# mLSTM stage: both parts of u are loaded from DRAM, where the pooling stage stores them, and the gates' bias is an eighth part of the gates' sum

## The chip, the cores and the metric

One core of a Trainium2 chip runs the program in one launch; times are device microseconds (us) of that core. TensorE (PE) multiplies, VectorE (DVE), ScalarE (ACT) and GpSimd (POOL) work on elements, and SyncE (SP) issues most of the DMA transfers. SBUF is the memory on the chip from which the engines read, PSUM the one into which PE writes.

## What is computed

A decoder layer over 4096 positions of width 1024. One normalised input u feeds two branches, a pooling mixer and an mLSTM with four heads; their outputs are joined, projected and added to x, and a last norm follows.

```python
def rmsnorm(x, w):
    y = x * lax.rsqrt(jnp.mean(x * x, axis=-1, keepdims=True) + EPS)
    return y * w

u = rmsnorm(x, norm_w)
proj = u @ w_in                      # 1024 x 5120: pool_x, pool_z, m_x, m_z, m_o
y_pool = pool_mixer(pool_x, pool_w, pool_scale) * silu(pool_z)
# mLSTM branch
xc = silu(causal_conv(m_x, conv_w, conv_b))
q, k, v = headwise(xc, w_q), headwise(xc, w_k), headwise(m_x, w_v)
gates = concatenate([q, k, v], -1) @ w_if + b_if     # 4 input and 4 forget gates
h = mlstm_chunkwise(q, k, v, i_pre, f_pre)           # chunks of 128, state C, n, m carried
y_mlstm = (head_norm(sigmoid(m_o) * h) * mh_norm_w + m_skip * xc) * silu(m_z)
out = rmsnorm(x + concatenate([y_pool, y_mlstm], -1) @ w_out, final_norm_w)
```

## The kernel before, in words

Products are taken in three matmuls each. A float32 operand is split into a high part, rounded to fp32r, and a low part, what is left (`split`, L104 casts on ACT and L105 subtracts, on DVE where no other engine is named), and `mm3` (L111 to L113) adds high by high, high by low and low by high.

The work has three parts in time.

*The pooling stage* goes through 8 blocks of 512 positions. For each block `norm_u` loads x transposed (x_t, L404), sums squares, has PE spread the norm (L419, L436) and stores the normalised x as float32 into the DRAM tensors us_d (L444), by quarters that later passes read. `make_u` splits it into the tiles u, eight pairs of a high and a low part, from a pool of 19 buffers. Eight steps j per block multiply u by two sets of weights (L111 to L113, `acc<-u,w`); the product is pooled, gated and stored to yp_d (L568). SP issues all these loads and stores in the order of its queue, and an issue waits there for the data it stores.

*The mLSTM stage* begins with its projection weights, eight pairs of loads of 256 KB with their splits (`ws`, L605), and with small products of the block-diagonal maps. Then `project(b)` computes m_x for sub-blocks of 256 positions, 16 of them. It loads the normalised x from us_d (L739, four loads of 256 KB) into tiles xu, casts the high part on ACT (L741) and subtracts on POOL (L742), in place. The pool xu has 12 tiles, of which one sub-block takes 8. The convolution and SiLU (`tail`, L678, L700 to L704) follow, and xc is stored to xc_d (L704).

`front` prepares a chunk of 128 positions: three products for v and its share of the gates (L779), each emptied by a split into va (L104, L105) and a reduction into `part` (L782); two maps for q and k (L789, copied by L791); two of scores (L800, emptied by L803 and L805); two transposes (L811). All of these take their PSUM from one ring of four buffers named `map`, in the order in which they are written. The gates g are the sum of the seven shares in `part` (L815) plus the bias `bif` (L816); ACT turns them into ef (L818 to L820), DVE into lf (L822), and PE transposes lf and g (L825, L826). `back` does the heads: it splits scaled rows into ws (L893 on ACT, L894 on DVE), multiplies by va and by the split state cs (L907, L911), stores h (L925 on ACT into ht, of which there is one buffer; L928) and updates the state c (L936, added by L937; its split on ACT and POOL is L665 and L666).

A string ORDER for even and one for odd chunks gives the order in which steps of `front`, `back`, `project` and `tail` are written. The framework's scheduler then orders the instructions of each engine by its own estimates, so a change of one instruction can move others. Two chunks, with one sub-block of `project`, make a period.

*The passes* after that form the output gate, the SiLU gate and the output projection (L1100 and later); the change leaves their code alone.

Of the kernel before, what the change touches and what calls it, by code (L numbers as in the profile page):

```python
# [8 lines left out]
F32 = mybir.dt.float32  # L9
F32R = mybir.dt.float32r  # L10
BF16 = mybir.dt.bfloat16
AF = mybir.ActivationFunctionType
ALU = mybir.AluOpType
# [4 lines left out]
P = 128  # L18
D = 1024
NJ = D // P  # L20

T = 512
# [5 lines left out]
TB = 256  # L28
# [12 lines left out]
A_OF = ("a11", "s2", "a12", "s3", "s1", "a22", "s4", "a21")  # L41
# [13 lines left out]
def tile_hybrid(  # L55
# [16 lines left out]
    nc = tc.nc  # L72
    S = x.shape[0]
    NB = S // T
# [5 lines left out]
    dram = ctx.enter_context(tc.tile_pool(name="dram", bufs=1, space=DRAM))  # L80
# [14 lines left out]
    us_d = [dram.tile([NP + 1, P, 4, T], F32, name=f"us_d{r}") for r in range(NR)]  # L95
    yp_d = [dram.tile([NP + 1, P, 4, T], F32, name=f"yp_d{r}") for r in range(NR)]
    ym_d = [dram.tile([NP, P, 4, T], F32, name=f"ym_d{r}") for r in range(NR)]
    xc_d = [dram.tile([NJ, P, T], F32, name=f"xc_d{b}") for b in range(NB)]
    h_d = [dram.tile([NCH, P, D], F32, name=f"h_d{b}") for b in range(NB)]

# [275 lines left out]
    def proj_t(ps, wpair, u):  # L376
        mm3(ps, [(kcol(wpair, k), u[k]) for k in range(NJ)])


    with tc.tile_pool(name="a_st", bufs=4) as stp, \  # L380
# [66 lines left out]
        def make_u(xs):  # L447
            u = []
            for k in range(NJ):
                hi = up.tile([P, T], F32R, name="u")  # L450
                lo = up.tile([P, T], F32R, name="u")
                split(xs[k // 2][:, k % 2], hi, lo)
                u.append((hi, lo))
            return u
# [70 lines left out]
        u = make_u(xs)  # L525
        job = None
        jobs = []
        for b in range(NB):
            if b % 2:
                jobs += [(us_d[b // 2], k) for k in (0, 2)]  # L530
            elif b:
                jobs += [(yp_d[b // 2 - 1], k) for k in (0, 2)]
            if b + 1 == NB:
                jobs += [(p_out1, k) for k in (0, 2)]
            for j in range(NJ):
                g = j // 2
                win = WINDOWS[g]
                ps = accp.tile([P, T], F32, name="acc")
                o = (j % 2) * P
                mm3(ps, [(tuple(t[:, k * 256 + o:k * 256 + o + P] for t in wz[g]), u[k]) for k in range(NJ)])  # L540
                z = wk.tile([P, HALO + T], F32, name="z")
                nc.scalar.copy(out=z[:, HALO:], in_=ps)
                nc.gpsimd.tensor_copy(out=z[:, 0:HALO], in_=halo[:, j, :])
                nc.gpsimd.tensor_copy(out=halo[:, j, :], in_=z[:, T:])
                pz = accp.tile([P, T], F32, name="acc")
                proj_t(pz, wg[j], u)
                sg = wk.tile([P, T], F32, name="sg")
                last_silu = nc.scalar.activation(out=sg, in_=pz, func=AF.Silu)

                cur, lo_c, step = z, 0, 1  # L550
                while step < win:
                    nxt = one.tile([P, HALO + T], F32, name=f"sum{(step.bit_length()) % 2}")
                    a = lo_c + step
                    nc.vector.tensor_tensor(out=nxt[:, a:], in0=cur[:, a:], in1=cur[:, a - step:HALO + T - step],
                                            op=ALU.add)
                    cur, lo_c, step = nxt, a, step * 2
                dlt = cur[:, HALO:]
                if b == 0:
                    n = win - 1
                    fix = wk.tile([P, HALO], F32, name="fix")  # L560
                    nc.vector.tensor_tensor(out=fix[:, :n], in0=cur[:, HALO:HALO + n], in1=inv0[:, :n], op=ALU.mult)
                nc.vector.scalar_tensor_tensor(out=dlt, in0=cur[:, HALO:], scalar=1.0 / win, in1=z[:, HALO:],
                                               op0=ALU.mult, op1=ALU.subtract)
                if b == 0:
                    nc.vector.tensor_tensor(out=dlt[:, :n], in0=fix[:, :n], in1=z[:, HALO:HALO + n], op=ALU.subtract)
                nc.vector.tensor_tensor(out=sg, in0=dlt, in1=sg, op=ALU.mult)
                quarter = A_OF.index(f"a{b % 2 + 1}{j // 4 + 1}")
                nc.sync.dma_start(out=yp_d[b // 2][quarter][:, j % 4, :], in_=sg)  # L568
                if b == 0 and j % 2 == 0 and g + 1 < H:
                    load_group(g + 1)  # L570
                if j == 0 and b + 1 < NB:
                    norm = norm_u(b + 1)
                if jobs and j in JOBS_AT[b + 1 == NB]:
                    dst, k = jobs.pop(0)
                    job = right_sums(dst, k) if dst is p_out1 else sums(dst, k)
                    next(job)
                elif job:
                    job = next(job, None)
                if j in NORM_AT[b > 0] and b + 1 < NB:
                    xs = next(norm)  # L580
            if b + 1 < NB:
                u = make_u(xs)
# [3 lines left out]
    with tc.tile_pool(name="b_mx", bufs=NJ) as mxp, \  # L586
# [7 lines left out]
        def x_tile(dt=F32):  # L594
            return xu.tile([P, T], dt, name="xu")

        def ws_tile():
            return wsp.tile([P, T], F32, name="ws")

        wm = [[w1p.tile([P, 4, T], F32R, name="w1") for _ in range(2)] for _ in range(4)]  # L600
        for i in range(4):
            for k in range(4):
                raw = ws_tile()
# [25 lines left out]
                                pattern=[[1, P]], channel_multiplier=-1)  # L629
        bif = one.tile([P, 8], F32, name="bif")  # L630
        nc.sync.dma_start(out=bif, in_=b_if.partition_broadcast(P))


        bvg = one.tile([P, NJ, GW], F32, name="bvg")
# [96 lines left out]
        def project(b):  # L731

            u = []
            for k in range(0, NJ, 2):
                lo = x_tile(F32R).rearrange("p (k l) -> p k l", k=2)
                raw = lo.bitcast(F32)
                l0 = b % 2 * TB
                quarter = A_OF.index(f"a{b // 2 % 2 + 1}{k // 4 + 1}")
                nc.sync.dma_start(out=raw, in_=us_d[b // 4][quarter][:, k % 4:k % 4 + 2, l0:l0 + TB])  # L739
                hi = x_tile(F32R).rearrange("p (k l) -> p k l", k=2)  # L740
                nc.scalar.copy(out=hi, in_=raw)  # L741
                nc.gpsimd.tensor_tensor(out=lo, in0=raw, in1=hi.bitcast(F32), op=ALU.subtract)  # L742
                u += [(hi[:, i], lo[:, i]) for i in range(2)]
            yield
            mx, xc = [], []
            for j in range(0, NJ, 2):
                ps = (accp if b or j % 4 else mmp).tile([P, 2, TB], F32, name="acc" if b or j % 4 else "mm")
                for i in range(2):
                    for part in range(2):
                        proj_part(ps[:, i], j + i, u, part)  # L750
                        if (i, part) != (1, 1):
                            yield
                m = mxp.tile([P, 2, 3 + TB], F32, name="mx", bufs=5)
                nc.gpsimd.tensor_copy(out=m[:, :, 0:3], in_=mhal[:, j:j + 2, :])
                nc.scalar.copy(out=m[:, :, 3:], in_=ps)
                nc.gpsimd.tensor_copy(out=mhal[:, j:j + 2, :], in_=m[:, :, TB:])
                a = mxp.tile([P, 2, TB], F32, name="xc", bufs=6)
                for t in range(2):
                    jj = j + t
                    nc.scalar.activation(out=a[:, t], in_=ps[:, t], func=AF.Identity,  # L760
                                         scale=conv_w[:, jj * 4 + 3:jj * 4 + 4], bias=conv_b[:, jj:jj + 1])
                tails.append(tail(b, j, m, a))
                mx += [m[:, i] for i in range(2)]
                xc += [a[:, i] for i in range(2)]
                if j + 2 < NJ:
                    yield
            return mx, xc

        def front(n, c, mx, xc):
            l0 = c * P  # L770
# [1 line left out]
            for t, one_ in zip(va, (1.0, 0.0)):  # L772
                nc.gpsimd.memset(t.bitcast(F32)[:, :, P:], one_)
            xs = st() if n + 1 < NB * NCH else None
            part = wk.tile([P, 8, 7], F32, name="part")
            for w, (j0, nj) in enumerate(((0, 3), (3, 3), (6, 2))):
                ps = mapp.tile([P, 3, GW], F32, name="map")
                for i in range(nj):
# [16 lines left out]
            for q in range(2):  # L795
                ps = mapp.tile([P, 2, GW], F32, name="map")
                for hh in range(2):
                    for t in range(2):
                        j = 4 * q + 2 * hh + t
# [4 lines left out]
                                        in1=causal.unsqueeze(1).broadcast_to([P, 2, P]), op=ALU.mult)  # L804
# [8 lines left out]
                yield  # L813
            g = wk.tile([P, 8], F32, name="g")
            nc.vector.tensor_reduce(out=g, in_=part, axis=AX.X, op=ALU.add)  # L815
            nc.vector.tensor_tensor(out=g, in0=g, in1=bif, op=ALU.add)  # L816
            ef = wk.tile([P, H], F32, name="ef")
            nc.scalar.activation(out=ef, in_=g[:, H:], func=AF.Abs)  # L818
            nc.scalar.activation(out=ef, in_=ef, func=AF.Exp, scale=-1.0)
# [55 lines left out]
            for h in range(H if n else 0):  # L875
                q = wk.tile([P, 2, 2, P], F32R, name="qi", bufs=4)
                raw = wk.tile([P, 2, P], F32, name="qr", bufs=4)
                nc.vector.tensor_tensor(out=raw, in0=qg[:, 2 * h:2 * h + 2, 0:P],
                                        in1=inter[:, h:h + 1, :].broadcast_to([P, 2, P]), op=ALU.mult)
# [426 lines left out]
```

## Time and profile before

| what | value |
|---|---|
| median of 3 runs | 3108.35 us (3103.76 to 3109.62) |
| profiled execution, its own time | 3106.23 us |
| its span | 3104.5 us |
| PE busy, mean granted clock | 2903.6 us (94%), 0.972 |
| DVE, ACT, POOL busy | 2116.8, 1352.9, 883.5 us |
| DMA | 531.59 MB, mean 171 GB/s |
| pooling stage | 0 to about 751 us |
| start of the mLSTM stage | about 751 to 815 us |
| mLSTM stage, steady part and end | about 815 to 1720 us |
| passes | to the end |

A row of waits reads: engine and line that waited, the engine and line that released it, then the total, the number and the longest wait in us. A row of the timeline is a start in us, a duration, the engine, the line and the tiles, and in brackets the idle time ahead of it. Rows of windows give the busy time of PE, of its weight loads, of DVE, ACT and POOL, then the granted clock, the DMA engines' share and GB/s.

### The profile page before, as it was taken

How to read it: one execution, taken by the hardware profiler on the slowest of the kernel's cores; microseconds unless marked ns; L12 is line 12 of the kernel's file. 1: busy time of each engine (PE TensorE's matmuls, PEld its weight loads, DVE VectorE, ACT ScalarE, POOL GpSimd, SP SyncE). 2: the span in 40 equal slices, each digit the busy share in tenths (PEclk: the TensorE clock that was granted, in tenths of full speed). 3: DMA queues.
4: the chain of work that ended last, by engine and by line, in shares of the span. 5: the costliest groups of instructions: out<-in, count | busy, mean ns of one | idle time of the engine just before them, and what ended most of it. 6: DMA issues, size and time to landing. Idle time of an engine off the chain costs nothing. (4 is left out here: it accounts for less than half of the span.)

```text
span 3104.5 us, 45002 instructions
## 1 busy us (share of the span) xinstructions
PE 2903.6 (94%) x15912; PEld 2520.3 (81%) x15912; DVE 2116.8 (68%) x4172; ACT 1352.9 (44%) x2658; POOL 883.5 (28%) x924
## 2 busy tenths in 40 slices
PE   7999999998899999999998898998999999989998
PEld 6888888887889989989997676886777778867887
DVE  6555555554688888888889644567667766676666
ACT  4222122221676676767767311245556633343332
POOL 1122333333244454444443231002011133220000
PEclk9999999998999999999999999999999999999999
DMA  6344455546221121111212788676677888886664
GB/s 214 113 158 157 160 186 187 186 149 199 82 67 50 49 69 49 61 57 48 66 59 92 250 281 288 218 256 218 228 238 247 268 270 279 277 285 207 202 210 169
DMA packets 258002, 531.59 MB, mean 171 GB/s; under 512 B 28528, under 2 KB 72048, under 8 KB 257776
## 3 DMA queue, kind: packets, MB, share of 16 engines
q1 hardware_dynamic: 225952, 412.84, 38.4%
q10 hardware_dynamic: 31824, 115.88, 12.2%
q8 instruction: 125, 2.05, 0.3%
q14 instruction: 101, 0.83, 0.1%
HBM read 331.49 MB, written 197.13 MB: 170 GB/s over the span
## 5 line engine op out<-in xcount | busy, mean ns | idle before, releaser
L111 PE MATMUL ps<-w,sr 128*128 128x512 f32 x1320 | 523.5, 397 | 27.0 <-ACT sr L104 18.5
L113 PE MATMUL ps<-w,sr 128*128 128x512 f32 x1320 | 520.4, 395 | 18.5 <-DVE sr L105 18.5
L112 PE MATMUL ps<-w,sr 128*128 128x512 f32 x1320 | 521.1, 395 | 0.0
L105 DVE TENSOR_TENSOR sr<-sr 128x1024 fp32r<-128x1024 f32 x221 | 284.9, 1292 | 302.2 <-ACT sr L104 301.5
L104 ACT CAST sr<-sr 128x1024 fp32r<-128x1024 f32 x221 | 231.2, 1047 | 535.0 <-PE ps L112 255.3
L111 PE MATMUL acc<-u,w 128*128 128x512 f32 x1024 | 399.3, 390 | 1.6 <-ACT u L104 1.6
L112 PE MATMUL acc<-u,w 128*128 128x512 f32 x1024 | 399.3, 390 | 0.0
L113 PE MATMUL acc<-u,w 128*128 128x512 f32 x1024 | 399.2, 390 | 0.0
L111 PEld LDWEIGHTS ps<-w,sr 128*128 128x128 f32 x1320 | 252.3, 191 | 82.2 <-ACT sr L104 22.3
L113 PEld LDWEIGHTS ps<-w,sr 128*128 128x128 f32 x1320 | 251.3, 190 | 74.5 <-DVE sr L105 22.2
L111 PE MATMUL acc<-xu,w 128*128 128x256 f32 x992 | 296.4, 299 | 0.0
L112 PEld LDWEIGHTS ps<-w,sr 128*128 128x128 f32 x1320 | 251.7, 191 | 52.4 <-issue 0.5
L113 PE MATMUL acc<-xu,w 128*128 128x256 f32 x992 | 283.3, 286 | 0.0
L112 PE MATMUL acc<-xu,w 128*128 128x256 f32 x992 | 283.3, 286 | 0.0
L666 POOL TENSOR_TENSOR cs<-c,cs 128x516 fp32r<-128x516 f32 x124 | 179.8, 1450 | 240.0 <-ACT cs L665 214.4
L678 DVE SCALAR_TENSOR_TENSOR xc<-mx,col,xc 128x256 f32<-128x256 f32 x384 | 226.2, 642 | 15.2 <-ACT xc L760 11.5
L111 PEld LDWEIGHTS acc<-u,w 128*128 128x128 f32 x1024 | 192.3, 188 | 42.3 <-ACT u L104 2.4
L113 PEld LDWEIGHTS acc<-u,w 128*128 128x128 f32 x1024 | 192.4, 188 | 40.1
L112 PEld LDWEIGHTS acc<-u,w 128*128 128x128 f32 x1024 | 192.4, 188 | 40.0
L111 PEld LDWEIGHTS acc<-xu,w 128*128 128x128 f32 x992 | 192.7, 194 | 1.2
L112 PEld LDWEIGHTS acc<-xu,w 128*128 128x128 f32 x992 | 192.8, 194 | 0.0
L113 PEld LDWEIGHTS acc<-xu,w 128*128 128x128 f32 x992 | 192.2, 194 | 0.1
(230 smaller groups left out, 5927.9 us busy)
## 6 DMA issues: line engine op xcount, KB each, us to landing
sr<-us_d ACTq DMA_DIRECT2D x112, 512.0 KB, 5.1
us_d<-st SPq DMA_DIRECT2D x64, 512.0 KB, 2.7
sr<-ym_d ACTq DMA_DIRECT2D x56, 512.0 KB, 4.3
sr<-yp_d ACTq DMA_DIRECT2D x53, 512.0 KB, 5.6
st<-in_x_t_dram SPq DMA_DIRECT2D x32, 512.0 KB, 6.0
yp_d<-sg SPq DMA_DIRECT2D x64, 256.0 KB, 2.9
st<-us_d SPq DMA_DIRECT2D x32, 512.0 KB, 5.9
xu<-us_d SPq DMA_DIRECT2D x64, 256.0 KB, 3.6
```

The costliest lines, as they stand in the source:

```text
L104: nc.scalar.copy(out=hi, in_=raw)
L105: (eng or nc.vector).tensor_tensor(out=lo, in0=raw, in1=hi.bitcast(F32), op=ALU.subtract)
L111: nc.tensor.matmul(ps, lhsT=a[0], rhs=b[0], start=start and k == 0, stop=False, skip_group_check=skip)
L112: nc.tensor.matmul(ps, lhsT=a[0], rhs=b[1], start=False, stop=False, skip_group_check=skip)
L113: nc.tensor.matmul(ps, lhsT=a[1], rhs=b[0], start=False, stop=stop and k == n - 1, skip_group_check=skip)
L666: nc.gpsimd.tensor_tensor(out=t[:, 1], in0=cst[h], in1=t[:, 0].bitcast(F32), op=ALU.subtract)
L678: nc.vector.scalar_tensor_tensor(out=a[:, t], in0=m[:, t, i:i + TB], scalar=conv_w[:, jj * 4 + i:jj * 4 + i + 1], in1=a[:, t], op0=ALU.mul ...
```

## The change

The pooling stage stores both parts of u to new DRAM tensors ub_d, one pair of stores for each j, behind the store of yp_d: 128 stores of 256 KB. `project` loads both parts from there, eight loads of 256 KB per sub-block in place of four; the cast L741 and the subtraction L742 are gone. `part` becomes two tiles that stay, used by even and odd chunks, with an eighth column that holds the bias, written once; the addition L816 is gone and L815 sums eight shares. us_d is still stored, since passes read it.

```diff
--- before.py
+++ after.py
@@ -95,6 +95,8 @@
     us_d = [dram.tile([NP + 1, P, 4, T], F32, name=f"us_d{r}") for r in range(NR)]
     yp_d = [dram.tile([NP + 1, P, 4, T], F32, name=f"yp_d{r}") for r in range(NR)]
     ym_d = [dram.tile([NP, P, 4, T], F32, name=f"ym_d{r}") for r in range(NR)]
+
+    ub_d = [dram.tile([2, P, NJ, T], F32, name=f"ub_d{b}") for b in range(NB)]
     xc_d = [dram.tile([NJ, P, T], F32, name=f"xc_d{b}") for b in range(NB)]
     h_d = [dram.tile([NCH, P, D], F32, name=f"h_d{b}") for b in range(NB)]
 
@@ -566,6 +568,8 @@
                 nc.vector.tensor_tensor(out=sg, in0=dlt, in1=sg, op=ALU.mult)
                 quarter = A_OF.index(f"a{b % 2 + 1}{j // 4 + 1}")
                 nc.sync.dma_start(out=yp_d[b // 2][quarter][:, j % 4, :], in_=sg)
+                for i in range(2):
+                    nc.sync.dma_start(out=ub_d[b][i][:, j, :], in_=u[j][i].bitcast(F32))
                 if b == 0 and j % 2 == 0 and g + 1 < H:
                     load_group(g + 1)
                 if j == 0 and b + 1 < NB:
@@ -629,6 +633,10 @@
                                 pattern=[[1, P]], channel_multiplier=-1)
         bif = one.tile([P, 8], F32, name="bif")
         nc.sync.dma_start(out=bif, in_=b_if.partition_broadcast(P))
+
+        gparts = [one.tile([P, 8, 8], F32, name=f"gp{i}") for i in range(2)]
+        for t in gparts:
+            nc.vector.tensor_copy(out=t[:, :, 7], in_=bif)
 
 
         bvg = one.tile([P, NJ, GW], F32, name="bvg")
@@ -732,14 +740,10 @@
 
             u = []
             for k in range(0, NJ, 2):
-                lo = x_tile(F32R).rearrange("p (k l) -> p k l", k=2)
-                raw = lo.bitcast(F32)
+                hi, lo = (x_tile(F32R).rearrange("p (k l) -> p k l", k=2) for _ in range(2))
                 l0 = b % 2 * TB
-                quarter = A_OF.index(f"a{b // 2 % 2 + 1}{k // 4 + 1}")
-                nc.sync.dma_start(out=raw, in_=us_d[b // 4][quarter][:, k % 4:k % 4 + 2, l0:l0 + TB])
-                hi = x_tile(F32R).rearrange("p (k l) -> p k l", k=2)
-                nc.scalar.copy(out=hi, in_=raw)
-                nc.gpsimd.tensor_tensor(out=lo, in0=raw, in1=hi.bitcast(F32), op=ALU.subtract)
+                for i, t in enumerate((hi, lo)):
+                    nc.sync.dma_start(out=t.bitcast(F32), in_=ub_d[b // 2][i][:, k:k + 2, l0:l0 + TB])
                 u += [(hi[:, i], lo[:, i]) for i in range(2)]
             yield
             mx, xc = [], []
@@ -772,7 +776,7 @@
             for t, one_ in zip(va, (1.0, 0.0)):
                 nc.gpsimd.memset(t.bitcast(F32)[:, :, P:], one_)
             xs = st() if n + 1 < NB * NCH else None
-            part = wk.tile([P, 8, 7], F32, name="part")
+            part = gparts[c % 2]
             for w, (j0, nj) in enumerate(((0, 3), (3, 3), (6, 2))):
                 ps = mapp.tile([P, 3, GW], F32, name="map")
                 for i in range(nj):
@@ -813,7 +817,6 @@
                 yield
             g = wk.tile([P, 8], F32, name="g")
             nc.vector.tensor_reduce(out=g, in_=part, axis=AX.X, op=ALU.add)
-            nc.vector.tensor_tensor(out=g, in0=g, in1=bif, op=ALU.add)
             ef = wk.tile([P, H], F32, name="ef")
             nc.scalar.activation(out=ef, in_=g[:, H:], func=AF.Abs)
             nc.scalar.activation(out=ef, in_=ef, func=AF.Exp, scale=-1.0)
```

Lines behind the first hunk move by two, later ones by three to eight: L605 becomes L609, L704 becomes L712, L739 becomes L746, L789 becomes L793, L936 becomes L939.

Three places in the order of instructions change. The first is PE in an odd chunk of the steady part, where `back`'s updates of two heads (mm<-va,ws), the projection (acc<-xu), the maps for q and k (map<-xc,bqk) and the first scores (map<-qg,xc) stand together. Before:

```order
L911 MATMUL mm<-cs,qi 128x258 x6
L936 MATMUL mm<-va_8747,ws 128x258
L936 MATMUL mm<-va_8748,ws 128x258
L936 MATMUL mm<-va_8747,ws 128x258 x2
L936 MATMUL mm<-va_8748,ws 128x258
L936 MATMUL mm<-va_8747,ws 128x258
L111 MATMUL acc<-xu,w_5571 128x256
L112 MATMUL acc<-xu,w_5571 128x256
L113 MATMUL acc<-xu,w_5572 128x256
L789 MATMUL map<-xc,bqk 128x128 x2
L800 MATMUL map<-qg,xc 128x136 x4
```

and now:

```order
L914 MATMUL mm<-cs,qi 128x258 x6
L939 MATMUL mm<-va_8853,ws 128x258
L939 MATMUL mm<-va_8854,ws 128x258
L939 MATMUL mm<-va_8853,ws 128x258
L793 MATMUL map<-xc,bqk 128x128 x2
L939 MATMUL mm<-va_8853,ws 128x258
L939 MATMUL mm<-va_8854,ws 128x258
L939 MATMUL mm<-va_8853,ws 128x258
L113 MATMUL acc<-xu,w_5707 128x256
L804 MATMUL map<-qg,xc 128x136 x4
L114 MATMUL acc<-xu,w_5707 128x256
```

Two of the map's matmuls moved in between the two heads' updates, and two of the three projection matmuls moved behind the scores.

The second is SP at the start of the mLSTM stage, where the last projection weights (ws) and the first loads of u stand. Before:

```order
L739 DMA xu<-us_d_72 128x2x256
L605 DMA ws<-in_w_in_dram 128x512
L739 DMA xu<-us_d_72 128x2x256
L605 DMA ws<-in_w_in_dram 128x512
L739 DMA xu<-us_d_72 128x2x256
L605 DMA ws<-in_w_in_dram 128x512 x2
L739 DMA xu<-us_d_72 128x2x256
L605 DMA ws<-in_w_in_dram 128x512
L739 DMA xu<-us_d_72 128x2x256
L605 DMA ws<-in_w_in_dram 128x512
L739 DMA xu<-us_d_72 128x2x256
L605 DMA ws<-in_w_in_dram 128x512 x2
```

and now:

```order
L609 DMA ws<-in_w_in_dram 128x512 x2
L746 DMA xu<-ub_d_84 128x2x256 x3
L609 DMA ws<-in_w_in_dram 128x512 x2
L746 DMA xu<-ub_d_84 128x2x256 x3
L609 DMA ws<-in_w_in_dram 128x512 x2
L746 DMA xu<-ub_d_84 128x2x256 x3
L609 DMA ws<-in_w_in_dram 128x512 x2
L746 DMA xu<-ub_d_84 128x2x256 x3
L609 DMA ws<-in_w_in_dram 128x512 x2
```

Loads of u come in threes between pairs of weights, where before one came at a time, and there are twelve of them ahead of the last pair for six.

The third is SP in the steady part, between the stores of h and of xc. Before:

```order
L928 DMA h_d_95<-ht 128x512
L704 DMA xc_d_88<-xc 128x2x256
L928 DMA h_d_95<-ht 128x512
L739 DMA xu<-us_d_74 128x2x256
L704 DMA xc_d_88<-xc 128x2x256
L928 DMA h_d_95<-ht 128x512
L739 DMA xu<-us_d_74 128x2x256 x2
L704 DMA xc_d_88<-xc 128x2x256
```

and now:

```order
L931 DMA h_d_102<-ht 128x512
L746 DMA xu<-ub_d_87 128x2x256
L712 DMA xc_d_95<-xc 128x2x256
L931 DMA h_d_102<-ht 128x512
L746 DMA xu<-ub_d_87 128x2x256 x3
L746 DMA xu<-ub_d_88 128x2x256 x4
L712 DMA xc_d_95<-xc 128x2x256
L931 DMA h_d_102<-ht 128x512
L712 DMA xc_d_95<-xc 128x2x256
```

The last three loads of one sub-block and the first four of the next stand in one row, where before two loads stood.

## The prediction

> **What bounds the kernel now.** I read the busy time by stretch first, then what TensorE (PE) waits for, then single instructions around the two waits that matter. The changed code runs in two stages. The row of a hundred microseconds stands for the pooling stage (0 to 751 us), the other for the steady part of the mLSTM stage (820 to 1640).
>
> ```profile
> 100.00:200.00 100.00, 100.00 (x443) 82.90 (x442) 59.39 (x82) 22.91 (x40) 27.03 (x26) 1.00 0.43 153
> 820.00:1640.00 820.00, 770.17 (x6279) 751.30 (x6278) 695.27 (x1937) 570.66 (x1372) 385.90 (x480) 0.98 0.18 57
> PE mm L936 <- DVE ws L894: 27.1, 13, 2.1
> PE map L825 <- DVE lf L822: 9.2, 14, 0.9
> ```
>
> In pooling PE is full (100.00 of 100) and the DMA engines are at 0.43: only what makes PE wait can cost there. In the mLSTM stage PE is busy 770.17 of 820, the transfers at 0.18 are far from a limit, and the 50 us that PE loses are small waits on DVE that return in each period of two chunks, some 14 times. No row names a load of u, so an earlier u is worth nothing by itself. What ends last there is DVE, and the question is whether the removed work delays DVE. The timeline of one period shows it (start, duration, engine, line):
>
> ```profile
> 1149.20 0.98 POOL L881 TENSOR_TENSOR qi<-qr,qi 128x256 fp32r<-128x256 f32 x1
> 1150.22 1.38 POOL L742 TENSOR_TENSOR xu<-xu 128x512 fp32r<-128x512 f32 x1
> 1150.38 1.89 DVE L678 SCALAR_TENSOR_TENSOR xc<-mx,col,xc 128x256 f32<-128x256 f32 x2
> 1152.59 0.87 DVE L894 SCALAR_TENSOR_TENSOR ws<-st,wcol,ws 128x256 fp32r<-128x256 f32 x2
> 1153.38 0.54 DVE L105 TENSOR_TENSOR va<-map,va 128x384 fp32r<-128x384 f32 x1
> 1153.85 0.17 DVE L782 TENSOR_REDUCE part<-map 128x8 f32<-128x24 f32 x1
> 1150.64 0.40 PE L936 MATMUL mm<-va,ws 128*128 128x258 f32 x2
> 1153.12 0.75 PE L936 MATMUL mm<-va,ws 128*128 128x258 f32 x4 [2.07 <-DVE ws L894]
> 1154.06 0.61 PE L789 MATMUL map<-xc,bqk 128*128 128x128 f32 x4
> ...
> 1161.63 0.21 DVE L815 TENSOR_REDUCE g<-part 128x8 f32<-128x56 f32 x1
> 1161.88 1.30 DVE L816 TENSOR_TENSOR g<-g,bif 128x8 f32<-128x8 f32 x1
> 1163.92 0.17 DVE L822 SCALAR_TENSOR_TENSOR lf<-g,ef 128x4 f32<-128x4 f32 x1 [0.75 <-ACT ef L820]
> 1161.87 1.29 POOL L742 TENSOR_TENSOR xu<-xu 128x512 fp32r<-128x512 f32 x1
> 1162.76 0.60 PE L811 MATMUL map<-ident,xc 128*128 128x128 f32 x4
> 1164.23 0.27 PE L825 MATMUL map<-ident,lf 128*4 128x128 f32 x1 [0.88 <-DVE lf L822]
> ```
>
> A DVE instruction that reads two SBUF operands while POOL runs a tensor_tensor stands until POOL is through. L816, a 128x8 add, begins 0.01 us behind the removed L742 and takes 1.30 instead of the 0.17 of its median:
>
> ```profile
> L816 DVE TENSOR_TENSOR g<-g,bif x29: 161/169/1301, 825.0 to 1620.8; 128x8 f32<-128x8 f32 x29
> L742 POOL TENSOR_TENSOR xu<-xu 128x512 fp32r<-128x512 f32 x56 | 74.7, 1334 | 53.3 <-ACT xu L741 52.1 <-DVE ws L894 0.5
> ```
>
> The page "SBUF — State Buffer" of the Trainium skill (section "SBUF: two separate sides") calls the port that these two engines share an exclusive lock, held for the whole instruction; the rows agree, since L816 ends at 1163.18 and L742 at 1163.16.
>
> The second loss is the clock. Windows cut where the granted clock changes, and two neighbouring periods (columns: PE, weight load, DVE, ACT, POOL busy, then PEclk):
>
> ```profile
> 1151.20:1154.60 3.40, 1.48 (x12) 1.48 (x13) 3.40 (x10) 1.90 (x4) 0.40 (x1) 1.00 0.00 0
> 1154.60:1158.02 3.42, 3.42 (x18) 3.42 (x17) 3.42 (x11) 2.68 (x6) 3.10 (x3) 0.50 0.10 34
> 1209.20:1212.60 3.40, 1.55 (x13) 1.55 (x14) 3.40 (x10) 1.97 (x4) 0.33 (x1) 1.00 0.00 0
> 1212.60:1216.00 3.40, 3.25 (x27) 3.04 (x27) 3.40 (x11) 2.94 (x7) 3.15 (x3) 1.00 0.11 36
> 1100.00:1157.90 57.90, 54.37 (x442) 53.14 (x442) 49.06 (x137) 40.05 (x96) 27.75 (x36) 0.97 0.17 56
> 1215.80:1272.00 56.20, 52.53 (x439) 51.10 (x437) 47.60 (x136) 39.35 (x96) 27.26 (x35) 1.00 0.18 56
> ```
>
> After a window in which PE idled 3.40 - 1.48 = 1.92 us the next 3.42 us run at half clock; after one with 3.40 - 1.55 = 1.85 they do not. The mean of 0.98 over 820 us is 16 us of lost clock, that is some 10 such windows at 3.42/2 = 1.7 us; the two periods differ by that same 57.9 - 56.2 = 1.7.
>
> **The change part by part.**
>
> *L742, L741 and L739 go (64 each); 128 direct loads come.* Where L742 overlaps nothing urgent its time is free. On the path it counts twice in a period.
>
> (a) Ahead of L936. The pair of L678 takes 1.89 under L742; an undisturbed pair of such instructions takes 0.87 (the two L894). So L894 comes 1.02 earlier and the wait of 2.07 becomes 1.05: -1.02.
>
> (b) What is late next. In the new order the first two L789 matmuls of the second map stand between two groups of three L936, where before they came behind all six and three matmuls of the projection. They write into the PSUM buffer that the first L105/L782 pair for va has to empty (a ring of four). That pair ends at 1153.85 + 0.17 = 1154.02, and by (a) at 1153.00. PE is there one matmul (0.13, since seven of them fill 1153.12 to 1154.06) behind the third L936, 1153.12 - 1.02 + 0.13 = 1152.23, so it waits 0.77, which it did not before: +0.77. The lower bound is 0 (if ACT or DVE reach the pair sooner), the upper 1.02, all of (a).
>
> (c) L816 goes too, as the bias becomes an eighth term of L815; its eight extra elements and the two copies at the start are bounded by L815's own 0.21 and are nothing. g is then ready at 1161.84 instead of 1163.18, 1.34 sooner, and PE's wait at L825, 0.88 here and 9.2/14 = 0.66 in the mean, is gone: -0.66 a period. In this chain ACT's ef stays, so that the last 0.46 of those 1.34 hide nothing.
>
> (d) The clock. In one window PE would now idle 1.05 + 0.77 = 1.82 at most, just below the 1.85 that kept full clock, and only if both waits fall into one window. I take 7 of the 10 half-clock windows as gone: -7 x 1.7 = -12, with bounds 0 and -17.
>
> The page "TensorE: Matmul & The Clock Gate" of the Trainium skill (section "HAM oscillation — how this bites in real kernels") gives the rule "no PE-idle gaps >~3.4µs". By it a gap of 2.07 would leave the clock alone, (d) would be 0 and the sum 12 us smaller; the rows show 0.50 behind that gap, so the trace speaks against the rule here.
>
> The steady part: 14 x (-1.02 + 0.77 - 0.66) = -12.7, and -12 for the clock.
>
> *Loads of u in the steady part.* SP now issues seven in a row, behind an xc_d and an h_d store, where before two stood:
>
> ```profile
> 1144.79 0.36 SPq L704 DMA_DIRECT2D xc_d<-xc  x1
> 1145.41 0.33 SPq L928 DMA_DIRECT2D h_d<-ht  x1
> 1145.85 1.12 SPq L739 DMA_DIRECT2D xu<-us_d  x2
> 1156.77 0.36 SPq L704 DMA_DIRECT2D xc_d<-xc  x1
> 1160.90 0.33 SPq L928 DMA_DIRECT2D h_d<-ht  x1
> ```
>
> Seven issues at 0.56 are done by about 1150, the next store comes at 1156.77 and ht, of which there is one buffer, has its store at 1160.90. The gap of ten microseconds is the cover; without it h_d would be late by the burst. I take 0.
>
> *The start of the mLSTM stage.* Here projection weights and u share SP. In the new order twelve loads of u stand between the last five pairs of weights, where before there were six:
>
> ```profile
> PE mm L111 <- ACT xu L741: 2.0, 1, 2.0
> PE mm L112 <- POOL xu L742: 1.5, 2, 0.8
> 785.00:790.00 5.00, 4.71 (x34) 4.22 (x33) 1.73 (x3) 2.48 (x4) 2.23 (x2) 0.90 0.62 177
> 790.00:795.00 5.00, 3.90 (x20) 3.29 (x20) 1.46 (x3) 2.48 (x4) 2.55 (x2) 0.78 0.73 220
> 793.26 2.44 SPq L605 DMA_DIRECT2D ws<-in_w_in_dram  x2
> ```
>
> The six loads more, of 256 KB at 220 GB/s, are 7 us. The waits on L741 and L742 (3.5 us) go with their instructions. If the loads are hidden that is -3.5, if none is +3.5, and +7 if the removed waits only hid behind the same transfers. PE is short of work there already (3.90 of 5 us), so I take a value nearer the dear end, +2.
>
> *The stores in the pooling stage.* 128 of 256 KB, 33.5 MB in 700 us, raise the DMA share from 0.43 by about 0.13 (48 GB/s at 153 GB/s for 0.43). They can only hurt through what SP issues behind them; the tightest is x_t for the next block, whose norm PE works on at L419 (the last row is from issue to landing of those loads, L404):
>
> ```profile
> 448.53 0.69 DVE L105 TENSOR_TENSOR sq<-ss,sq 128x512 fp32r<-128x512 f32 x1
> 454.54 0.64 PE L419 MATMUL tp<-sq,ones_r 128*128 128x512 f32 x2
> DMA to landing us min/median/max: 4.7/6.1/7.1
> ```
>
> Slack is 454.54 - 449.22 = 5.3 us. Two to four stores ahead of it are 0.4 us each to issue and 0.5 to 1.0 MB to move, 2 to 5 us at worst. I take 0.
>
> Sum: -12.7 - 12 + 2 = -22.7. The profiled execution took 3106.23 (its span 3104.5 and 1.7 around it), so 3083.5; against the median of 3108.35, 2.1 us above it, 3085.7. I forecast **3086 us**.
>
> **The rivals.**
>
> *The clock stays (chance 0.15).* The new idle of 1.82 is 0.03 from the 1.85 that stayed clear, and a small shift tips it. Then the sum is -10.7, or with L789's wait at its upper bound (+1.02 for +0.77, 3.5 us in all) -7.2: 3098 to 3101. The rule of the Trainium skill's page "TensorE: Matmul & The Clock Gate" (section "HAM oscillation — how this bites in real kernels"), by which such gaps leave the clock alone, ends at the same -10.7. For it: 1.05 and 0.77 lie within 2 us of each other. Against: a window boundary falls between them in over half of the phases.
>
> *L789 does not wait (0.13).* If ACT or the scheduler frees the PSUM buffer earlier, (b) is 0 and all 10 windows keep full clock: -14 x 1.68 - 17 + 2 = -38.5, 3070. Against it: the pair stands behind both L894 on DVE in the new order too.
>
> *L742's time was covered anyway (0.14).* Removing it lets L666 and L881 of POOL move into the freed places and stretch the same DVE rows (L881 at 1149.20 already lies over one L678), so that (a) and (d) vanish and only part of (c) is left, -14 x 0.3 + 2 = -2.2: within 0.2%, 3106. For it: POOL keeps over 80% of its time here, since L742 is 74.7 of 385.90. Against it: those two wait on ACT, not on L742.
>
> *The x_t chain breaks (0.10, slower).* If the u stores queue ahead of the x_t loads of all six blocks in which PE waits for nothing now, and delay them beyond 5.3 us, PE stands at L419 in each block. The deciding point is a delay over 5.3 us. Four stores in flight plus one more round of 512 KB landing (6.1) make a delay of some 11 us, so 5.7 x 6 = 34 us lost and, less the 22.7 gained, +11: 3120. Against it: the stores lie at 0.43 of the DMA's share, and the 2 to 5 us above.
>
> **How the numbers follow.** Forecast 0.48, clock 0.15, no wait at L789 0.13, covered 0.14, slower 0.10. What a measurement can tell from no change is 0.2%, 6.2 us. Faster: 0.48 + 0.15 + 0.13 = 0.76, with 0.01 lost to the edge of the clock rival, 0.75. Same: 0.14 + 0.01, and 0.01 from the slower case, 0.16. Slower: 0.09. The likeliest case has its own range of 3078 to 3094, from 14 x 0.2 us for (b), two windows either way for (d) and the start. For 8 in 10 the range takes the clock rival and most of the third rival on one side, and the 3070 on the other: 3068 to 3105.
>
> **What would show it.** The wait of L936 on L894 at some 1 us instead of 2.07, with L678's longest near 1 us; a new wait of PE at L789 (now L793) on L105 or L782 of 0.8 us; no row for L825 on L822; PEclk of 0.99 or 1.00 in 820 to 1640; periods of 56 us; in the pooling stage PE at 100.00 and its end within 2 us of 751. I am wrong if L936 still waits 2 us (then L742 was not what held L678), if half-clock windows are as many as before, or if PE shows a wait at L419.

## The result

The changed kernel takes 3060.18 us (median of 4 runs, 3059.04 to 3064.14) against 3108.98 us of the kernel before on the same chip: ratio 0.9845, 95% interval 0.9833 to 0.9857. That is 48.8 us faster, more than twice the 22.7 us that I had summed, and below my range, which ended at 3068. Its profiled execution took 3060.25, its span is 3058.5.

Its waits of PE in the steady part of the mLSTM stage (engine and line, released by; total us, times, longest), and the busy time of its pooling and steady parts (PE, weight loads, DVE, ACT, POOL, then the granted clock, DMA share, GB/s):

```profile
PE mm L939 <- DVE ws L897: 13.8, 13, 1.1
PE mm L910 <- DVE c L940: 9.4, 15, 0.9
PE mm L910 <- DVE st L107: 1.0, 1, 1.0
...
PE map L828 <- DVE lf L825: 0.4, 2, 0.2
...
100.00:200.00 100.00, 100.00 (x443) 82.93 (x442) 57.40 (x81) 23.63 (x41) 27.37 (x26) 1.00 0.55 197
815.00:1600.00 785.00, 759.21 (x6326) 742.93 (x6325) 660.96 (x1927) 550.28 (x1326) 308.32 (x425) 1.00 0.25 80
```

The same stretch of the kernel before:

```profile
815.00:1600.00 785.00, 736.21 (x6007) 717.77 (x6006) 666.48 (x1856) 544.94 (x1307) 368.46 (x455) 0.98 0.17 56
```

The wait for ws (L936 before, L939 now) fell from 2.1 to 1.1 us each, the wait for lf (L825, now L828) from 9.2 us in all to 0.4, and the mean granted clock of the stretch rose from 0.98 to 1.00. The pooling stage is as full as it was, with the DMA share at 0.55 for 0.43.

Where the 46.0 us between the two spans went is seen from the starts of one instruction, the transpose of lf, of which there is one for each of the 32 chunks. The rows give minimum, median and maximum duration in ns, then the first and the last start; the first is of before, the second of the changed kernel:

```profile
L825 PE MATMUL map<-ident,lf x32: 269/270/271, 826.7 to 1708.5; 128*4 128x128 f32 x32
```

```profile
L828 PE MATMUL map<-ident,lf x32: 269/272/273, 823.0 to 1663.1; 128*4 128x128 f32 x32
```

Up to the first chunk 3.7 us are gained; from the first to the last 881.8 becomes 840.1, that is 41.7 us; behind the last 1396.0 becomes 1395.4, 0.6 us. The gain lies in the mLSTM stage. I call the stretch from first to last transpose the chunk stretch below and compare kernels by it, since what lies behind it, the passes, differs between executions (1386.9 to 1403.3 us over the thirteen profiles).

### The profile page after: what moved, and what is told of

It reads as the page before. It is cut to its first block, busy times and chain, and to the rows that moved or that the text cites. A ratio compares the mean times of both kernels' runs of the same rounds, so it can differ in the third digit from the quotient of the medians.

```text
span 3058.5 us, 45082 instructions
## 1 busy us (share of the span) xinstructions
PE 2888.9 (94%) x15912; PEld 2507.7 (82%) x15912; DVE 2054.6 (67%) x4142; ACT 1323.2 (43%) x2594; POOL 793.3 (26%) x860
## 5 line engine op out<-in xcount | busy, mean ns | idle before, releaser
L107 DVE TENSOR_TENSOR sr<-sr 128x1024 fp32r<-128x1024 f32 x221 | 284.9, 1292 | 298.2 <-ACT sr L106 290.6
L674 POOL TENSOR_TENSOR cs<-c,cs 128x516 fp32r<-128x516 f32 x124 | 174.9, 1410 | 311.7 <-ACT cs L673 287.7
L686 DVE SCALAR_TENSOR_TENSOR xc<-mx,col,xc 128x256 f32<-128x256 f32 x384 | 207.6, 593 | 13.8 <-ACT xc L764 11.4
```

The lines of the kernel that those rows point to most:

```text
L107: (eng or nc.vector).tensor_tensor(out=lo, in0=raw, in1=hi.bitcast(F32), op=ALU.subtract)
L674: nc.gpsimd.tensor_tensor(out=t[:, 1], in0=cst[h], in1=t[:, 0].bitcast(F32), op=ALU.subtract)
L686: nc.vector.scalar_tensor_tensor(out=a[:, t], in0=m[:, t, i:i + TB], scalar=conv_w[:, jj * 4 + i:jj * 4 + i + 1], in1=a[:, t], op0=ALU.mul ...
```

## The experiments

My theory was the prediction's: POOL's subtraction for u (L742) stretches DVE instructions on which PE waits, and PE's idle time in these waits halves the clock behind them. Against it stood that the bias is worth as much, that the cast which ACT no longer does, or the new order of PE, brings the gain, and that stores or loads cost something.

**The bias alone.** In the kernel before:

```diff
...
-            part = wk.tile([P, 8, 7], F32, name="part")
+            part = gparts[c % 2]
...
-            nc.vector.tensor_tensor(out=g, in0=g, in1=bif, op=ALU.add)
```

> The kernel before, with only the bias moved into the gates' sum (L816 gone; the cast and the POOL subtraction of u stay). Theory (POOL's subtraction stretches DVE, and the idle that this makes halves the clock): PE's wait for lf goes (9.2 us in all), the wait of 2.1 us for ws stays and with it some ten half-clock windows: 9 to 12 us faster, 3097 to 3100. Rival (the shorter chain of the gates is worth as much as the loads): 20 us or more, below 3090.

3091.36 us, ratio 0.9946 (0.9921 to 0.9971). That is a gain of 17 us, between the theory's 9 to 12 and the rival's 20, and nearer to the rival's. The profiled execution is at 3097.73 and shows what stayed:

```profile
PE mm L939 <- DVE ws L897: 25.1, 12, 2.1
PE mm L910 <- DVE c L940: 8.9, 14, 0.9
PE map L828 <- DVE lf L825: 5.2, 8, 1.6
...
815.00:1600.00 785.00, 740.34 (x6049) 721.78 (x6049) 661.05 (x1845) 550.49 (x1319) 369.67 (x459) 0.98 0.17 57
```

The wait for ws is untouched and so is the clock of 0.98. The wait for lf is not gone, since POOL's subtraction (L746 here) now stretches the next instruction of that chain, the one that makes lf. It takes 0.16 us in the median and 0.98 here:

```profile
L825 DVE SCALAR_TENSOR_TENSOR lf<-g,ef x29: 156/164/985, 824.5 to 1614.6; 128x4 f32<-128x4 f32 x29
...
874.22 1.26 POOL L746 TENSOR_TENSOR xu<-xu 128x512 fp32r<-128x512 f32 x1 [0.42 <-ACT xu L745]
874.52 0.98 DVE L825 SCALAR_TENSOR_TENSOR lf<-g,ef 128x4 f32<-128x4 f32 x1 [0.73 <-ACT ef L823]
```

In this profile the wait for lf is 4.0 us shorter than before and the chunk stretch 6.5 us (875.3 for 881.8). The five executions split: 3096.99 and 3097.73 us at a mean clock of 0.972 and 0.973, and 3089 to 3091 at 0.975 to 0.977, where thirteen executions of the kernel before, run beside them, had 0.967 to 0.973. So part of the 17 us goes with a higher clock, that is with fewer half-clock windows, whose number differs from one execution to the next. How much of it the bias itself gives is not shown. Why three executions had a higher clock than any of before, I can't say, as the profiled one is not among them.

**The loads alone.** The stores and loads of both parts, with L816 kept:

```diff
...
-                nc.scalar.copy(out=hi, in_=raw)
-                nc.gpsimd.tensor_tensor(out=lo, in0=raw, in1=hi.bitcast(F32), op=ALU.subtract)
+                for i, t in enumerate((hi, lo)):
+                    nc.sync.dma_start(out=t.bitcast(F32), in_=ub_d[b // 2][i][:, k:k + 2, l0:l0 + TB])
```

> The kernel before, with only the stores and loads of both parts of u (the bias is still added by a DVE instruction of its own). Theory: without POOL's subtraction that addition takes 0.17 us in place of 1.30, so most of the wait for lf goes as well, and with the waits for ws and the half-clock windows gone the gain is 40 to 47 us of the 48: 3062 to 3069. Rival (two separate gains that add up): 48 less the gain of the bias alone, that is about 38 us, 3070 or more if the bias alone gives 10.

3063.02 us, ratio 0.9851 (0.9821 to 0.9881), within the theory's span. The loads alone bring nearly all of it, and the two parts do not add up: 17 and 46 us apart, 49 together. The wait for lf goes without the bias being moved:

```profile
PE mm L935 <- DVE ws L893: 14.0, 13, 1.3
...
PE map L824 <- DVE lf L821: 0.4, 2, 0.3
```

**The cast put back, without POOL.** In the changed kernel, a cast on ACT that nobody reads, for each pair of u tiles:

```diff
+                nc.scalar.copy(out=idle[0], in_=hi.bitcast(F32))
```

> The changed kernel, with the ACT cast of 128x512 put back for every pair of u tiles, into a tile that nobody reads; POOL has no subtraction. PE's order goes back near to that of before. Theory: ACT and PE's order are not what counts, so the gain stays: 3058 to 3068, the wait for ws near 1.1 us. Rival (the cast that ACT no longer does, and the order that came with it, bring the gain): 3090 or more.

3068.7 us, ratio 0.9864 (0.9841 to 0.9887), 0.7 us over the theory's span. The gain stays but for 8.5 us. The wait for ws is as in the changed kernel, and the loss has a row of its own, PE waiting for ACT's copy of the maps, together with an order of PE close to that of before:

```profile
PE mm L942 <- DVE ws L900: 13.8, 13, 1.1
PE mm L913 <- DVE c L943: 8.8, 14, 0.9
PE map L807 <- ACT qg L798: 7.7, 13, 1.1
```

**POOL's subtraction put back, without the cast.** PE's order stays that of the changed kernel:

```diff
+                nc.gpsimd.tensor_tensor(out=idle, in0=hi.bitcast(F32), in1=lo.bitcast(F32), op=ALU.subtract)
```

> The changed kernel, with POOL's subtraction of 128x512 put back for every pair of u tiles (its result is read by nobody), without the cast; PE's order is the changed kernel's own. Theory: the subtraction stretches the same DVE instructions, so the wait for ws is 2 us or more again, the half-clock windows are back, and most of the gain is lost: 3090 to 3112. Rival (ACT or the order brought the gain): 3058 to 3068.

3097.75 us, ratio 0.9966 (0.9948 to 0.9983). Over three quarters of the gain is lost (37.6 of 48.8 us). In the profiled execution (3105.44) the chunk stretch is back at 883.3 us, for 840.1 in the changed kernel and 881.8 before. The wait for ws in its steady part, one period of it, and the busy times:

```profile
PE mm L942 <- DVE ws L900: 25.5, 13, 3.2
...
1155.81 2.80 POOL L749 TENSOR_TENSOR idle<-xu 128x512 f32<-128x512 f32 x2 [1.22 <-DMA xu<-ub_d]
1155.98 2.90 DVE L900 SCALAR_TENSOR_TENSOR ws<-st,wcol,ws 128x256 fp32r<-128x256 f32 x2
1157.52 0.39 PE L942 MATMUL mm<-va,ws 128*128 128x258 f32 x1 [2.06 <-DVE ws L900]
...
815.00:1600.00 785.00, 738.76 (x5984) 719.87 (x5983) 658.80 (x1822) 517.90 (x1246) 366.70 (x455) 0.97 0.23 74
```

Two subtractions that POOL does for nobody lie on the pair L900 (in the kernel before, one lay on L678 just ahead of it), which takes 2.90 us where it took 0.87 undisturbed; PE waits 2.06 us, and the clock falls to 0.97. The wait for lf stays away (0.8 us in all), which fits that not the whole gain is lost. With the run of the cast this shows the theory: it is POOL's subtraction that cost most; ACT's cast and the order that comes with it cost no more than the 8.5 us above.

**The stores alone.** In the kernel before, the 128 stores are added and read by nobody:

```diff
+                for i in range(2):
+                    nc.sync.dma_start(out=ub_d[b][i][:, j, :], in_=u[j][i].bitcast(F32))
```

> The kernel before, with only the 128 stores of both parts of u added in the pooling stage (nobody reads them). Theory: they lie beside a full PE and reach nothing that waits, so within 0.2% of before, and PE at 100.00 of every 100 us from 100 to 740. Rival (they delay the loads of x_t past their slack): PE waits at the norm's matmul in each block, 10 to 35 us slower.

3110.91 us, ratio 1.0006 (0.9994 to 1.0017). They cost nothing that can be measured; PE is busy 640.00 of the 640 us from 100 to 740.

**The idle filled.** In the kernel before, PE gets ten needless matmuls ahead of the update that waits:

```diff
+                    for _ in range(10 * (c % 2 == 1 and h + t == 0)):
+                        nc.tensor.matmul(upd, lhsT=xw[h][:, 0, t * P:(t + 1) * P], rhs=vh[0], start=True, stop=True)
```

> The kernel before, with ten extra matmuls of 128x258 in every odd chunk, written into the PSUM buffer ahead of the first update of the state, which overwrites them; their operands are there before the wait for ws, so they fill about 1.2 us of PE's wait of 2.1 us. Theory (idle of about 2 us within one clock window halves the clock for the next): the half-clock windows of this stage go, and the kernel gets 8 to 17 us faster by doing more work: 3091 to 3101. Rival (such a gap leaves the clock alone, and the half-clock windows come from elsewhere): no change or slower, 3106 to 3125.

3110.74 us, ratio 1.0008 (0.9998 to 1.0018), so by the time the rival's number. The profile gives half of each:

```profile
PE map L825 <- DVE lf L822: 11.1, 15, 0.8
PE mm L938 <- DVE ws L894: 10.9, 12, 0.9
PE mm L907 <- DVE c L939: 9.2, 14, 0.9
PE map L789 <- DVE xc L703: 8.6, 12, 0.7
PE map L789 <- ACT qg L791: 4.7, 13, 0.4
...
815.00:1600.00 785.00, 736.06 (x6065) 713.65 (x6064) 658.85 (x1837) 539.68 (x1297) 366.17 (x452) 1.00 0.17 55
```

With 0.9 us of idle left in the wait for ws the clock is 1.00: the half-clock windows do follow PE's idle. But PE's order changed with the ten matmuls, L789 came earlier and waits 13.3 us in all, and nothing was left of the gain; the chunk stretch is even 9.4 us longer (891.2 for 881.8). What the rest of that loss is, I did not follow. So this run shows the cause of the windows and not their price.

**The state's rows split earlier.** I tried to take away the 1.1 us that is left of the wait for ws, with four ws buffers for two and the first two heads' split written ahead of the masked scores:

```diff
...
+            xw = [prep(xs, wcol, h) for h in range(2)] if xs is not None else []
             nc.vector.scalar_tensor_tensor(out=dm, in0=dm, scalar=3e38, in1=sc, op0=ALU.min, op1=ALU.mult)
...
-                prep(0)
-                prep(1)
```

> The changed kernel, with the split of the first two scaled heads (ACT, then DVE, 0.87 us) written ahead of the masked scores instead of behind the chunk, and four ws buffers instead of two: on DVE it now stands before the six instructions of the convolution that it stood behind. Theory (what is left of the wait for ws, 1.06 us a period, is DVE's time in those six): that wait goes in 13 or 14 periods, 3044 to 3052. Rival (the split of the scores, which now comes 0.87 us later on DVE, takes its place as the wait of the next matmuls): 3056 to 3064.

3094.89 us, ratio 0.9959 (0.9946 to 0.9972): 35 us slower than the changed kernel, which neither expected. The wait for ws is gone from the rows, and PE waits elsewhere instead:

```profile
PE map L812 <- DVE gp L794: 14.0, 13, 1.4
PE map L801 <- DVE xc L711: 11.4, 12, 1.0
```

The clock is 1.00 here too, so it is not the clock. My reading, which no run tests, is that the DVE instructions that now stand behind the split are later by what it takes, and that PE's order moved with it: the wait was moved up in the queue of a full engine and came back at other places. What the remaining loss consists of, I did not follow.

**POOL's other subtractions on DVE.** If a subtraction on POOL costs DVE its time anyway, DVE may as well do it. In the changed kernel, first for one head of four, then for all:

```diff
-                nc.gpsimd.tensor_tensor(out=q[:, 1], in0=raw, in1=q[:, 0].bitcast(F32), op=ALU.subtract)
+                (nc.vector if h == H - 1 else nc.gpsimd).tensor_tensor(out=q[:, 1], in0=raw,
+                                                                       in1=q[:, 0].bitcast(F32), op=ALU.subtract)
```

> The changed kernel, with one of POOL's four subtractions for qi in a chunk (that of the last head, which lies over the convolution's DVE instructions) moved to DVE. Theory (POOL's subtractions cost DVE more than they take off it): the six convolution instructions get 0.5 to 1.0 us shorter, the moved one takes 0.43 us of that back, so the wait for ws falls from 1.06 to some 0.6: 3050 to 3058. Rival (DVE is full there, and what it does itself comes on top): 3062 to 3075.

3047.9 us, ratio 0.981 (0.9778 to 0.9842), 2 us under the theory's span. The wait for ws, 13.8 us in the changed kernel, is nearly gone:

```profile
PE mm L940 <- DVE ws L898: 0.3, 1, 0.3
```

All four:

```diff
-                nc.gpsimd.tensor_tensor(out=q[:, 1], in0=raw, in1=q[:, 0].bitcast(F32), op=ALU.subtract)
+                nc.vector.tensor_tensor(out=q[:, 1], in0=raw, in1=q[:, 0].bitcast(F32), op=ALU.subtract)
```

> The changed kernel, with all four subtractions for qi in a chunk moved from POOL to DVE. Theory: DVE gains back about as much as it takes on (4 x 0.43 us against stretches that sum to about 2.5 us in two chunks), 3050 to 3065. Rival (DVE is full, 3.4 us of work more in a period): 3085 to 3110.

3045.4 us, ratio 0.9804 (0.9778 to 0.983), better than either expected, and not told apart from the run with one. Once more, with more executions:

> The changed kernel with all four subtractions for qi on DVE, once more and in more rounds, for its interval beside the changed kernel: 3040 to 3050 by what one job has shown of it; 3055 or more if that job was favoured by where the clock's windows fell.

3044.79 us, ratio 0.9797 (0.9777 to 0.9818). The interval lies below that of the changed kernel, so this version beats both kernels, by about 15 us over the changed one (0.0048 of 3108). Its rows:

```profile
PE mm L910 <- DVE c L940: 9.5, 15, 0.9
PE map L793 <- ACT qg L795: 2.6, 14, 0.4
PE map L828 <- DVE lf L825: 1.5, 3, 1.1
...
1128.58 2.45 DVE L686 SCALAR_TENSOR_TENSOR xc<-mx,col,xc 128x256 f32<-128x256 f32 x6
1130.96 0.74 DVE L884 TENSOR_TENSOR qi<-qr,qi 128x256 fp32r<-128x256 f32 x2
1131.63 0.86 DVE L897 SCALAR_TENSOR_TENSOR ws<-st,wcol,ws 128x256 fp32r<-128x256 f32 x2
...
815.00:1600.00 785.00, 770.58 (x6402) 752.70 (x6403) 679.15 (x2064) 555.62 (x1339) 196.12 (x314) 1.00 0.25 82
```

In the changed kernel the six L686 of that place take 3.41 us, here 2.45:

```profile
1131.09 3.41 DVE L686 SCALAR_TENSOR_TENSOR xc<-mx,col,xc 128x256 f32<-128x256 f32 x6
1132.05 0.98 POOL L884 TENSOR_TENSOR qi<-qr,qi 128x256 fp32r<-128x256 f32 x1
```

The wait for ws has no row any more. DVE's busy time rose by only 18 us (660.96 to 679.15), although it took over 112 subtractions, for which POOL had needed 103.4 us.

The last step moves the subtraction for cs as well (L674, 128x516):

> The same, with the subtraction for the split state cs (128x516) moved from POOL to DVE as well, so that POOL has no two-operand work left in this stage. Theory (each POOL subtraction costs DVE as much as doing it would): DVE takes on 110 x 0.8 = 88 us and gets back the 50 us or so that its instructions still stretch; with DVE busy 680 of 785 that is 720, still under PE's 770, and PE loses only where the order changes: 3040 to 3060. Rival (DVE is the bound from here): 3065 or more.

3055.39 us, ratio 0.9826 (0.9801 to 0.985): inside the theory's span, and no better than the step before.

```profile
PE acc L113 <- ACT xc L764: 3.4, 13, 0.5
PE map L861 <- DVE parts L859: 2.1, 6, 1.2
...
L674 DVE TENSOR_TENSOR cs<-c,cs 128x516 fp32r<-128x516 f32 x112 | 76.8, 686 | 9.2 <-ACT cs L673 7.6
...
815.00:1600.00 785.00, 776.04 (x6368) 753.49 (x6367) 681.51 (x2161) 557.89 (x1332) 40.06 (x202) 1.00 0.24 80
```

DVE took on 76.8 us of L674, and its busy time rose by 2.4 us only (679.15 to 681.51), where I had expected 720. Part of that came back from instructions that POOL no longer stretches: L686 took 178.4 us in the step before and takes 150.7 now. PE is busy 776.04 of 785 and hardly waits, yet its chunk stretch is 835.1 us against 827.0 in the step before (821.5 to 1656.6 against 823.9 to 1650.9). The clock is 1.00 in both. The order of all engines is another one here, and why a busier PE gets through less, I leave open.

## Why the prediction was wrong

**(a) the wait for ws: right.** I expected 1.05 us for 2.07; the rows have 13.8/13 = 1.06. One sign that I had named did not come: the longest L678 (now L686) was to be near 1 us, and it is still 1.53, three times the median.

```profile
L686 DVE SCALAR_TENSOR_TENSOR xc<-mx,col,xc x347: 466/474/1529, 814.7 to 1599.8; 128x256 f32<-128x256 f32 x174
```

POOL's other subtractions lie over the long ones, L674 (128x516) at other places of the period and L884 at this one, as the last runs above bear out.

**(b) the wait at L789: wrong, +10.8 us that never came.** I had PE wait 0.77 us in each period, for a PSUM buffer that the first L105/L782 pair empties. One period of the changed kernel (L793 is the map, L107 the split of va):

```profile
1134.96 0.39 PE L939 MATMUL mm<-va,ws 128*128 128x258 f32 x1 [1.08 <-DVE ws L897]
1135.18 0.60 PE L793 MATMUL map<-xc,bqk 128*128 128x128 f32 x4
1135.22 0.55 DVE L107 TENSOR_TENSOR va<-map,va 128x384 fp32r<-128x384 f32 x1
```

L793 begins without a wait, 0.04 us ahead of the very instruction that I had it wait for. It does not use that buffer: in the compiled program the second map takes the buffer of the first, which ACT's copy (L795) empties. I had counted buffers round a ring in the order of the code, and took it for support that in the profile of before L789 came 0.04 us behind the pair (1154.06 and 1154.02); that was chance. The compiled order lists the wait of this matmul, and it names ACT alone:

```
L793 MATMUL map<-xc,bqk 128x128 [waits Activation_49]
```

It could have been read before. The rival "L789 does not wait", to which I gave 0.13, was the true case: 3070 by its sum.

**(c) the wait for lf: right in size, not in cause.** It went (9.2 us to 0.4). But the loads alone do it (0.4), and the bias alone takes 4.0 of the 9.2 us: the 1.30 us of L816 were POOL's, as the prediction's own row had shown, and I still booked them under the bias.

**(d) the clock: right in kind, mis-sized.** I took 7 of 10 half-clock windows as gone; of the ten that the profile of before has between 820 and 1640 us, the changed kernel has one, near the start of the stage:

```profile
826.20:829.60 3.40, 3.40 (x19) 3.40 (x18) 2.38 (x9) 1.89 (x3) 0.00 (x0) 0.50 0.00 0
```

Over the whole chunk stretch there were fourteen such windows of 3.41 us and there are four now. At half of 3.41 us each, that is 17.1 us, where I had booked 12. I had held some back because (b) would have brought the idle to 1.82 us of a window. My price of 1.7 us a window came from two periods, and it fits the spread of the executions: a straight line through time and mean clock of thirteen executions of the kernel before falls by 3.1 us for each 0.001 of clock, and 0.001 of 3108 us is 3.1.

**The steady part in one sum:** 10.8 from (b) and 5 from (d) are 15.8 of the 17.0 us by which the chunk stretch beat my 24.7.

**The start: wrong by 5.7 us, and not settled.** I took +2, the profile has -3.7. The waits there are as long as before, on other rows (3.5 us for L741 and L742 before; now 1.9 for a weight and 1.4 for a load of u). The longest wait there, for the weights of the maps, is 11.7 us for 12.9, and the half-clock time between 755 and 797 us is 30.7 us for 34.1, one window less:

```profile
PE mm L113 <- ACT w L106: 1.9, 1, 1.9
PE mm L114 <- DMA xu<-ub_d: 1.4, 1, 1.4
```

The first transpose of lf came at 821.5 to 826.7 us (mean 824.4) in the eight profiles with the new loads and the old place of the split, and at 824.9 to 827.7 (mean 826.1) in the four with the old loads. That is some 2 us gained, within what executions differ; the loads between the weights cost nothing that shows.

**The x_t chain and the h_d stores: right.** PE is full through the pooling stage, and no row of a wait names either. The first block ended 1.8 us later, by a half-clock window and not by a store: the clock of the first 50 us, 1.00 before, is now 0.97, and 0.03 of 50 us is 1.5. The run of the filled idle, without any of these stores, has the same 0.97, and the run of the stores alone has 1.00. The rows are of the changed kernel and of the filled idle:

```profile
0.00:50.00 50.00, 33.53 (x132) 27.19 (x133) 31.80 (x54) 23.97 (x40) 6.66 (x14) 0.97 0.74 248
...
0.00:50.00 50.00, 32.81 (x132) 26.82 (x133) 33.24 (x57) 26.13 (x44) 6.70 (x14) 0.97 0.75 246
```

**The range.** It left 3060 out because I had taken (b) for the likeliest and let only one rival without it reach the low end. A wait that is inferred from how buffers should be counted, and that no row shows, should have had its lower end in the range together with that of the clock and of the start. By my own bounds that is -23.5 - 17 - 3.5 = -44 us, 3064: nearer, and still 4 us above what came.

## What to carry to other kernels

Work done on POOL was not off DVE here where both read two operands from SBUF: look, at each place where PE waits for DVE, at what POOL does in the same microsecond, and compare the long instruction with the median of its line. Take a wait for a buffer from the compiled order's waits, not from counting buffers in the source. An idle of about 2 us on PE cost nearly as much again here in the clock behind it (1.7 us), so the sum of a small wait may need a second term.

## What was not expected of the hardware

Half-clock windows came behind less idle than the profile of before had suggested. There, 1.85 us of idle in a window left the clock alone; in the run with POOL's subtraction put back, 3.42 - 1.67 = 1.75 us did not:

```profile
1098.39:1101.81 3.42, 1.67 (x12) 1.26 (x12) 3.42 (x8) 2.88 (x6) 2.07 (x2) 1.00 0.98 334
1101.81:1105.22 3.41, 3.41 (x16) 3.41 (x17) 3.41 (x13) 0.60 (x2) 3.41 (x3) 0.50 0.16 57
```

So the threshold is not a sharp number of idle microseconds as these rows count them. The Trainium skill's page "TensorE: Matmul & The Clock Gate" (section "HAM oscillation — how this bites in real kernels") puts it at gaps above about 3.4 us; every run here that waits 2 us in each period has a mean clock of 0.97 or 0.98 in the steady part, and those without such waits have 1.00, so the measurements here speak against that rule. The page "SBUF — State Buffer" of the Trainium skill (section "SBUF: two separate sides") says that the one that comes second is blocked for the other's whole instruction; the pair L900 above, 2.90 us under 2.80 us of POOL for 0.87, agrees.
